# Modulation rows split between TensorE and VectorE, and two narrow projections in 32-column groups

## Chip, core and metric

One Trainium2 chip, one core of it. The program is one launch over all inputs, in fp32. The metric is the device time of one execution in microseconds; several executions of the kernel are timed and the median is taken.

## What is computed

A first block (a gated delta rule and a spatial gating unit, then a mixture of experts) and a second block of two layers (forgetting attention, latent attention, each with a mixture of experts), over 512 tokens of 1024 channels. Three pieces of it are touched:

```python
# second block: 2 layers x 6 vectors of 1024, from one vector c
c_act = jax.nn.silu(c)                       # (1, 1024)
mod = c_act @ w_ada[i] + b_ada[i]            # w_ada[i] is (1024, 6144): 50 MB in two layers
sh1, sc1, g1, sh2, sc2, g2 = jnp.split(mod, 6, axis=-1)

# first block: 16 narrow columns of the input projection
proj = x @ w_in                              # a, b: 8 columns each, from 4096
beta = sigmoid(b);  g = -exp(a_log) * softplus(a + dt_bias)

# forgetting attention: 16 narrow columns
f_logit = (h @ fox_w_in)[..., 3 * D:]        # log_f = log_sigmoid(f_logit + b_f)
```

## The kernel before

The program is laid out by hand in phases, and a scheduling layer then orders the instructions of each engine. Engines run their own queue in that order, so an instruction that waits holds up all behind it on its engine. The phase in question is the first mixer (the first 716 us): spatial gating (`sgu`), then the delta rule (`delta`, with a triangular inverse on VectorE, `sgu_out`, and a scan over chunks), then `gated_sum`.

Nearly all matrix products are exact in fp32 by a split: a weight tile `st` is loaded by SyncE's queue, ScalarE writes its high part `wh` (fp32r), GpSimd or VectorE the rest `wl` (L222), and `mm3` (L384 to L386) adds three fp32r products. A step of `weight1` is 24 such matmuls of 512 moving columns (or 48 of 256). Products in plain fp32 also occur, and the profile shows them as two records each, one for each of two passes (L1259, L1614, L1784).

**Modulation** (`modulation`, L1581 to L1620) is a generator that `weight1` advances: 80 calls, every fifth two steps, 96 steps in all. A step handles one 128-row block k of `w_ada` for one of the 12 vectors: a 512 KB tile `ast` (128 x 1024) from SyncE's queue, of which three are in flight (`AHEAD = 3`, three buffers). VectorE forms `acc = ast * ca[k]` at k = 0 (L1607) and `acc += ast * ca[k]` at k = 1 to 7 (L1609), with `ca` = silu(c) down the partitions. After k = 7 two TensorE products of a column of ones sum `acc` over the partitions into one bank of kind "gen" (L1614, in column groups at output partitions 0 and 32), VectorE adds the bias row (L1618) in two parts of one partition each, and ScalarE's queue writes the vector to DRAM (L1619). The load of step n + 3 is issued behind step n, since it reuses that step's buffer.

**Narrow projections** (`narrow`, L686 to L705) load a weight strip, padded to 64 columns in `gates` and 16 in `fox_heads`, split it in two parts, and take 24 products with the strip as the stationary operand; ScalarE copies the result out and four transposes turn it.

**PSUM.** Eight banks, dealt out by kind in rotation. In the first mixer kind "mm" has banks 0 to 5, in `delta` banks 0 to 2. A bank may be written again when its last reader is done: in `delta` that is VectorE for the convolutions (L722) and for `sgu_out` (L628), ScalarE elsewhere.

Of the kernel before, what the change touches and what calls it, by code (L numbers as in the profile page):

```python
# [10 lines left out]
F32 = mybir.dt.float32  # L11
F32R = mybir.dt.float32r
# [3 lines left out]
AF = mybir.ActivationFunctionType  # L16
ALU = mybir.AluOpType
AX = mybir.AxisListType
# [3 lines left out]
P = 128  # L22
D = 1024
KD = D // P
S = 512
NT = S // P
AHEAD = 3
# [4 lines left out]
def f32(ap):  # L32
    return ap.bitcast(F32)
# [89 lines left out]
class Net:  # L123
# [308 lines left out]
    def mixer1(self):  # L432
        nc, tc, io = self.nc, self.tc, self.io
        ctx = ExitStack()
        with ctx:
# [3 lines left out]
            with ExitStack() as c1:  # L439
                self.wpools(c1, 3, ahead=2, size=1024)  # L440
                self.t2s(c1, x=16)
                self.psums(mm=(0, 1, 2, 3, 4, 5), gen=(6, 7))
                x = io["x"][0]
                xin = self.big("xin")
                for t in range(NT):
                    nc.scalar.dma_start(xin[:, t, :], x[t * P:(t + 1) * P, :])
                self.stage()
                self.slots_left = 0
                self.ada = self.modulation(self.pool(c1, "ada", 1))
                self.xT = self.transpose_split([xin[:, t, :] for t in range(NT)], lambda n, d: self.t2("x", d))  # L450
                with ExitStack() as c2:
                    self.t2s(c2, u=8, gt=2)
                    gT = self.sgu()
                    self.delta_consts()
                    with ExitStack() as c3:
                        self.angles(self.pool(c3, "ang", 1, side="right"))
                    self.head_consts()
                    self.logits = Logits(self, self.t2, io["router_group_w"][0], io["router_group_b"][0],
                                         io["router_expert_w"][0], io["router_expert_b"][0], io["ln1_g"][0], None,
                                         io["ln1_b"][0], True)  # L460
                self.psums(mm=(0, 1, 2), sc=(3, 4, 5), gen=(6,), tr=(7,))
                with ExitStack() as c2:
                    self.t2s(c2, kT=8, th=3, e=2, er=2, qv0=4)
                    self.delta(gT)
                self.psums(mm=(0, 1, 2, 3, 4, 5), gen=(6, 7))
                with ExitStack() as c2:
                    self.t2s(c2, sg=8, ysl=4)
                    y = self.gated_sum()
                    for _ in self.ada:
                        pass  # L470
# [212 lines left out]
            last = self.nc.vector.scalar_tensor_tensor(o, o, mv[:, 1:2], b[i], op0=ALU.mult, op1=ALU.add)  # L683
        return last

    def narrow(self, alloc, parts, n, xT):  # L686

        nc = self.nc

        def tile3(name, dt):  # L690
            return alloc(name, dt, KD * n)[:, :KD * n].rearrange("p (k c) -> p k c", k=KD)

        st, wh, wl = tile3("nw", F32), tile3("nwh", F32R), tile3("nwl", F32R)
        nc.gpsimd.memset(st, 0.0)
        for src, o in parts:
            nc.gpsimd.dma_start(st[:, :, o:o + src.shape[1]], src.rearrange("(k p) c -> p k c", p=P))
        self.split(wh, wl, st)
        ps = self.mm_ps()
        self.ws(ps[:n], ([wh[:, k, :] for k in range(KD)], [wl[:, k, :] for k in range(KD)]), 0, n, xT)
        ab = alloc("nab", F32, S)[:n]  # L700
        nc.scalar.activation(ab, ps[:n], AF.Copy)
        pt = self.mm_ps()
        for t in range(NT):
            nc.tensor.transpose(pt[:, t * n:(t + 1) * n], ab[:, t * P:(t + 1) * P], self.ident[:n, :n])
        return pt[:, :NT * n].rearrange("p (t c) -> p t c", t=NT)  # L705


# [29 lines left out]
    def gates(self):  # L737
        nc, io, sc = self.nc, self.io, self.sc
        w_in = io["w_in"][0]
        pv = self.narrow(lambda n, d, m: self.t2("u", d), [(w_in[:, 4096:4104], 0), (w_in[:, 4104:4112], 32)], 64, self.xT)  # L740
        dtb = self.bcast_row(sc, io["dt_bias"][0], 8, "dtb")
        ea = self.bcast_row(sc, io["a_log"][0], 8, "ea")
        self.tc.keep_in_program_order(nc.scalar.activation(ea, ea, AF.Exp))
# [5 lines left out]
        nc.scalar.activation(self.beta, pv[:, :, 32:40], AF.Tanh, scale=0.5)  # L749
# [830 lines left out]
    def modulation(self, ap):  # L1580

        nc, io = self.nc, self.io
        self.mods = self.dr.tile([2, 6, D], F32, name="mods")
        ca = ap.tile([P, KD], F32, name="ca")
        nc.gpsimd.dma_start(ca, io["c_2"][0].rearrange("(k p) -> p k", p=P))
        nc.scalar.activation(ca, ca, AF.Silu)
        steps = [(l, m, k) for l in range(2) for m in range(6) for k in range(KD)]
        tiles = {}

        def load(n):  # L1590

            if n < len(steps):
                l, m, k = steps[n]
                tiles[n] = ap.tile([P, D], F32, tag="ast", name=self.name("ast"), bufs=AHEAD)
                nc.sync.dma_start(tiles[n], io["w_ada_2"][l, k * P:(k + 1) * P, m * D:(m + 1) * D])

        for n in range(AHEAD):
            load(n)
        for n, (l, m, k) in enumerate(steps):
            st = tiles.pop(n)  # L1600
            if k == 0:
                acc = ap.tile([P, D], F32, tag="acc", name=self.name("acc"), bufs=1)
                row = ap.tile([P, 512], F32, tag="row", name=self.name("row"), bufs=1)
                for i in range(2):
                    nc.gpsimd.dma_start(row[32 * i:32 * i + 1, :],
                                        io["b_ada_2"][l:l + 1, m * D + i * 512:m * D + (i + 1) * 512])
                nc.vector.tensor_scalar(acc, st, ca[:, 0:1], None, op0=ALU.mult)  # L1607
            else:
                nc.vector.scalar_tensor_tensor(acc, st, ca[:, k:k + 1], acc, op0=ALU.mult, op1=ALU.add)  # L1609
            load(n + AHEAD)  # L1610
            if k == KD - 1:
                ps = self.ps("gen")
                for i in range(2):
                    nc.tensor.matmul(ps[32 * i:32 * i + 1, :], self.ones[:, 0:1], acc[:, i * 512:(i + 1) * 512],  # L1614
                                     start=True, stop=True)
                for i in range(2):
                    r = slice(32 * i, 32 * i + 1)
                    nc.vector.tensor_tensor(row[r, :], row[r, :], ps[r, :], op=ALU.add)  # L1618
                    nc.scalar.dma_start(self.mods[l, m:m + 1, i * 512:i * 512 + 512], row[r, :])  # L1619
            yield  # L1620

    def mod_row(self, pool, l, m):
# [219 lines left out]
    def fox_heads(self, ctx, l, x, finish, rows, w_in, op):  # L1842
# [17 lines left out]
        with ExitStack() as c2:  # L1860
# [15 lines left out]
            self.logits = self.logits_of(np_, l)  # L1876

            pf = self.narrow(lambda n, d, m: np_.tile([P, m], d, name=self.name(n)),
                             [(w_in[:, 3072:3088], 0)], 16, xT)
# [300 lines left out]
```

## Time and profile before

| | |
|---|---|
| median of 3 timed executions | 2050.21 us (2049.0 to 2052.03) |
| profiled execution | 2048.78 us, of which 2047.0 us is its span |
| granted TensorE clock, mean | 0.944 |
| TensorE busy | 1821.6 us, 89% of the span |
| VectorE busy | 1376.9 us, 67% |
| ScalarE, GpSimd busy | 857.7 us (42%), 522.6 us (26%) |

A busy share counts an engine's instructions from start to end; matmul ends are modelled and overlap the next start, so how fast TensorE proceeds is read from the starts of following rows. Idle time that the profile puts down to a releaser is named in the views of waits. The two passes of an fp32 product are two rows or two counts.

### The profile page before, as it was taken

How to read it: one execution, taken by the hardware profiler on the slowest of the kernel's cores; microseconds unless marked ns; L12 is line 12 of the kernel's file. 1: busy time of each engine (PE TensorE's matmuls, PEld its weight loads, DVE VectorE, ACT ScalarE, POOL GpSimd, SP SyncE). 2: the span in 40 equal slices, each digit the busy share in tenths (PEclk: the TensorE clock that was granted, in tenths of full speed). 3: DMA queues.
4: the chain of work that ended last, by engine and by line, in shares of the span. 5: the costliest groups of instructions: out<-in, count | busy, mean ns of one | idle time of the engine just before them, and what ended most of it. 6: DMA issues, size and time to landing. Idle time of an engine off the chain costs nothing. (4 is left out here: it accounts for less than half of the span.)

```text
span 2047.0 us, 30174 instructions
## 1 busy us (share of the span) xinstructions
PE 1821.6 (89%) x11594; PEld 1531.3 (75%) x11594; DVE 1376.9 (67%) x2482; ACT 857.7 (42%) x1610; POOL 522.6 (26%) x404
## 2 busy tenths in 40 slices
PE   6989987798889985999589999969997799987997
PEld 6878766677777775888478998957886677786885
DVE  2786885767775466565757555567768778566776
ACT  3334311223333223665334546325543376633552
POOL 5342335223434311111310001231214100232212
PEclk9989999899999987999799998979998999998999
DMA  8753456352547563997404111549972410337993
GB/s 233 191 169 128 154 161 213 101 157 95 152 137 231 178 239 133 330 354 259 162 22 124 42 63 44 225 157 343 357 253 100 135 35 21 118 151 282 349 357 142
DMA packets 174728, 363.33 MB, mean 177 GB/s; under 512 B 23086, under 2 KB 114814, under 8 KB 162288
## 3 DMA queue, kind: packets, MB, share of 16 engines
q1 hardware_dynamic: 154544, 317.94, 46.8%
q0 software_dynamic: 16528, 32.83, 4.7%
q10 hardware_dynamic: 3504, 10.54, 1.3%
q8 instruction: 94, 1.54, 0.3%
q14 instruction: 58, 0.48, 0.1%
HBM read 337.45 MB, written 47.25 MB: 188 GB/s over the span
## 5 line engine op out<-in xcount | busy, mean ns | idle before, releaser
L227 ACT ACTIVATE wh<-st 128x1024 fp32r<-128x1024 f32 (+2 forms) x283 | 310.6, 1101 | 304.3 <-PE mm L386 89.9
L222 DVE TENSOR_TENSOR wl<-st,wh 128x1024 fp32r<-128x1024 f32 (+3 forms) x202 | 263.5, 1306 | 87.3 <-ACT wh L227 86.6
L222 POOL TENSOR_TENSOR wl<-st,wh 128x1024 fp32r<-128x1024 f32 (+1 forms) x81 | 209.0, 2585 | 293.7 <-ACT wh L227 236.8
L384 PE MATMUL mm<-wh,xeh 128*128 128x256 f32 x720 | 211.8, 294 | 0.0
L385 PE MATMUL mm<-wl,xeh 128*128 128x256 f32 x720 | 203.6, 283 | 0.0
L386 PE MATMUL mm<-wh,xel 128*128 128x256 f32 x720 | 203.5, 283 | 0.0
L384 PE MATMUL mm<-x,wh 128*128 128x512 f32 x448 | 183.7, 410 | 15.1 <-DVE sy L628 12.8
L386 PE MATMUL mm<-x,wl 128*128 128x512 f32 x448 | 182.8, 408 | 0.0
L385 PE MATMUL mm<-x,wh 128*128 128x512 f32 x448 | 182.3, 407 | 0.0
L1609 DVE SCALAR_TENSOR_TENSOR acc<-ast,ca,acc 128x1024 f32<-128x1024 f32 x84 | 140.2, 1669 | 62.5 <-DMA ast<-in_w_ada_dram 61.5
L1259 PE MATMUL down<-st,hT 128*128 128x512 f32 x384 | 174.3, 596 | 1.9 <-ACT hT L227 1.9
L385 PEld LDWEIGHTS mm<-wl,xeh 128*128 128x128 f32 x720 | 137.9, 191 | 0.7 <-issue 0.7
L384 PEld LDWEIGHTS mm<-wh,xeh 128*128 128x128 f32 x720 | 137.5, 191 | 0.8 <-issue 0.7
L386 PEld LDWEIGHTS mm<-wh,xel 128*128 128x128 f32 x720 | 137.6, 191 | 0.0
L1274 POOL DMA_INDIRECT yd<-ye,rows x42 | 42.2, 1004 | 318.2 <-DVE ye L1271 185.0
L1259 PEld LDWEIGHTS down<-st,hT 128*128 128x128 f32 x384 | 69.1, 190 | 71.5 <-issue 68.9
L384 PEld LDWEIGHTS mm<-x,wh 128*128 128x128 f32 x448 | 87.0, 194 | 38.1 <-issue 19.6
L384 PE MATMUL mm<-wh,fXH 128*128 128x256 f32 x384 | 113.9, 297 | 0.0
L386 PE MATMUL mm<-wh,fXL 128*128 128x256 f32 x384 | 110.3, 289 | 1.8 <-DVE fXL L222 1.8
L385 PE MATMUL mm<-wl,fXH 128*128 128x256 f32 x384 | 111.0, 289 | 0.0
L385 PEld LDWEIGHTS mm<-x,wh 128*128 128x128 f32 x448 | 86.9, 194 | 17.3 <-issue 1.7
L386 PEld LDWEIGHTS mm<-x,wl 128*128 128x128 f32 x448 | 87.3, 195 | 16.2
(558 smaller groups left out, 4660.0 us busy)
## 6 DMA issues: line engine op xcount, KB each, us to landing
ast<-in_w_ada_dram SPq DMA_DIRECT2D x96, 512.0 KB
st<-in_w_in_dram SPq DMA_DIRECT2D x32, 1024.0 KB
st<-in_moe_w_gate_dram SPq DMA_DIRECT2D x32, 1024.0 KB
st<-in_moe_w_up_dram SPq DMA_DIRECT2D x32, 1024.0 KB
st<-in_moe_w_down_dram SPq DMA_DIRECT2D x30, 1024.0 KB
st<-in_expert_w_gate_dram SPq DMA_DIRECT2D x16, 1024.0 KB
st<-in_expert_w_up_dram SPq DMA_DIRECT2D x16, 1024.0 KB
st<-in_expert_w_down_dram SPq DMA_DIRECT2D x15, 1024.0 KB
```

The lines of the kernel that those rows point to most:

```text
L222: rest = eng.tensor_tensor(l, src, f32(h), op=ALU.subtract)
L227: return self.nc.scalar.activation(out, in_, AF.Copy)
L384: mm(out, lh, rh, start=(start and i == 0), stop=False)
L385: mm(out, lh, rl, start=False, stop=False)
L386: last = mm(out, ll, rh, start=False, stop=(stop and i == n - 1))
L1259: self.nc.tensor.matmul(ps[i], hT[:, k * P:(k + 1) * P], w[:, k * D + i * 512:k * D + (i + 1) * 512], start=k == 0, stop=k == 1)
L1274: return self.nc.gpsimd.indirect_dma_start(out=self.yd[:, :], out_offset=bass.IndirectOffsetOnAxis(ap=dst, axis=0), in_=ye, in_offset=None ...
L1609: nc.vector.scalar_tensor_tensor(acc, st, ca[:, k:k + 1], acc, op0=ALU.mult, op1=ALU.add)
```

## The change

The modulation's even blocks (k = 0, 2, 4, 6) go to TensorE: for each, four fp32 matmuls whose stationary operand is `ca[k]` repeated in 32 columns, over 256 moving columns each, into the four 32-partition groups of one bank. That bank (2, kind "ada") is kept for it through the first mixer, so "mm" has five banks there and two in `delta`. The odd blocks stay on VectorE: k = 1 starts `acc` (tensor_scalar), k = 3, 5, 7 add to it. After k = 7 the ones product (now 32 columns, four groups) adds `acc` to the same bank; one VectorE addition over 128 partitions x 256 columns adds the bias, which now comes as a row repeated in each group, and one DMA writes the vector. Only two loads are issued ahead, with three buffers: the load of step n + 2 stands behind step n and reuses the buffer of step n - 1.

`narrow` keeps its strip in fp32, with no split: 32 columns wide for both uses, eight k blocks in two sets of four, each k block of a set in its own column group, over the high and then the low part of x: 16 fp32 matmuls of 512 moving columns in place of 24. The four partial sums are added in the turning step, which becomes four fp32 products with a 128 x 32 selector (made by one VectorE reduction) in place of four transposes.

```diff
-                self.psums(mm=(0, 1, 2, 3, 4, 5), gen=(6, 7))
+                self.psums(mm=(0, 1, 3, 4, 5), gen=(6, 7), ada=(2,))
...
-                self.psums(mm=(0, 1, 2), sc=(3, 4, 5), gen=(6,), tr=(7,))
+                self.psums(mm=(0, 1), sc=(3, 4, 5), gen=(6,), tr=(7,), ada=(2,))
...
-        st, wh, wl = tile3("nw", F32), tile3("nwh", F32R), tile3("nwl", F32R)
+        st = alloc("nw", F32, KD * n)[:, :KD * n].rearrange("p (k c) -> p k c", k=KD)
...
-        self.split(wh, wl, st)
+        sel = alloc("nsel", F32, n)[:, :n]
+        nc.vector.reduce_sum(sel, self.ident.rearrange("p (g c) -> p c g", g=4), axis=AX.X)
         ps = self.mm_ps()
-        self.ws(ps[:n], ([wh[:, k, :] for k in range(KD)], [wl[:, k, :] for k in range(KD)]), 0, n, xT)
-        ab = alloc("nab", F32, S)[:n]
-        nc.scalar.activation(ab, ps[:n], AF.Copy)
+        for k0 in (0, 4):
+            for i, x in enumerate(xT):
+                for g in range(4):
+                    nc.tensor.matmul(ps[n * g:n * g + n, :], st[:, k0 + g, :], f32(x[k0 + g]),
+                                     start=k0 + i == 0, stop=k0 + i == 5)
+        ab = alloc("nab", F32, S)
+        nc.scalar.activation(ab, ps, AF.Copy)
         pt = self.mm_ps()
         for t in range(NT):
-            nc.tensor.transpose(pt[:, t * n:(t + 1) * n], ab[:, t * P:(t + 1) * P], self.ident[:n, :n])
+            nc.tensor.matmul(pt[:, t * n:(t + 1) * n], ab[:, t * P:(t + 1) * P], sel, start=True, stop=True)
...
+        def rows(ps, w, src, start, stop):
+
+            for a in range(4):
+                nc.tensor.matmul(ps[32 * a:32 * a + 32, :], w, src[:, a * 256:(a + 1) * 256], start=start, stop=stop)
+
-        for n in range(AHEAD):
+        for n in range(AHEAD - 1):
             load(n)
...
             if k == 0:
+                ps = self.ps("ada")[:, :256]
+                row = ap.tile([P, 256], F32, tag="row", name=self.name("row"), bufs=2)
...
-                nc.vector.tensor_scalar(acc, st, ca[:, 0:1], None, op0=ALU.mult)
+            if k % 2 == 0:
+                rows(ps, ca[:, k:k + 1].to_broadcast([P, 32]), st, k == 0, False)
+            elif k == 1:
+                nc.vector.tensor_scalar(acc, st, ca[:, k:k + 1], None, op0=ALU.mult)
             else:
                 nc.vector.scalar_tensor_tensor(acc, st, ca[:, k:k + 1], acc, op0=ALU.mult, op1=ALU.add)
-            load(n + AHEAD)
+            load(n + AHEAD - 1)
             if k == KD - 1:
-                ps = self.ps("gen")
-                for i in range(2):
-                    nc.tensor.matmul(ps[32 * i:32 * i + 1, :], self.ones[:, 0:1], acc[:, i * 512:(i + 1) * 512],
-                                     start=True, stop=True)
-                for i in range(2):
-                    r = slice(32 * i, 32 * i + 1)
-                    nc.vector.tensor_tensor(row[r, :], row[r, :], ps[r, :], op=ALU.add)
-                    nc.scalar.dma_start(self.mods[l, m:m + 1, i * 512:i * 512 + 512], row[r, :])
+                rows(ps, self.ones[:, 0:32], acc, False, True)
+                nc.vector.tensor_tensor(row, row, ps, op=ALU.add)
+                nc.scalar.dma_start(self.mods[l, m].rearrange("(a c) -> a c", a=4),
+                                    row.rearrange("(a b) c -> a b c", a=4)[:, 0, :])
```

The scheduling layer orders all engines anew. Three places are shown; `st`, `ast`, `acc`, `sy` and `row` are the tiles named above, `X` and `Y` the inverse matrices, `q` a small operand that GpSimd prepares, `qv` the convolutions, `sc` scan banks, and numbers count buffers.

On TensorE, before, where the first product with X stands (`join`, L933), late in the third convolution's 24 matmuls:

```order
L386 MATMUL mm_3122<-x_183,wl_3027 128x512
L384 MATMUL mm_3122<-x_192,wh_3026 128x512
L385 MATMUL mm_3122<-x_193,wh_3026 128x512
L386 MATMUL mm_3122<-x_192,wl_3027 128x512
L933 MATMUL sc_2746<-X_2722,q_2738 128x128 x4
L384 MATMUL mm_3122<-x_201,wh_3026 128x512
```

The same place now (that product is L937 here, the convolutions are mm_3097, mm_3142, mm_3182):

```order
L385 MATMUL mm_3142<-x_202,wh_2734 128x512
L386 MATMUL mm_3142<-x_201,wl_2735 128x512
L1604 MATMUL ada_3084<-ast_3140,ca 32x256 x4
L1604 MATMUL ada_3084<-ast_3225,ca 32x256 x4
L937 MATMUL sc_2800<-X_2776,q_2792 128x128 x4
L384 MATMUL mm_3182<-x_138,wh_3080 128x512
```

The third convolution moved behind the first product with X, and two modulation blocks, each behind the load of its tile, stand in its place.

On VectorE, before, the rows that lead to the transposes which build X and Y (L912, L913):

```order
L1618 TENSOR_TENSOR row_2469<-row_2469,gen_2688 1x512 x2
L1607 TENSOR_SCALAR acc_3030<-ast_2616,ca 128x1024
L1609 SCALAR_TENSOR_TENSOR acc_3030<-ast_2650,ca,acc_3030 128x1024
L1609 SCALAR_TENSOR_TENSOR acc_3030<-ast_2686,ca,acc_3030 128x1024
L628 SCALAR_TENSOR_TENSOR sy_2643<-sy_2643,mm_2695 128x512
L1609 SCALAR_TENSOR_TENSOR acc_3030<-ast_3035,ca,acc_3030 128x1024
L1609 SCALAR_TENSOR_TENSOR acc_3030<-ast_3038,ca,acc_3030 128x1024
L912 STREAM_TRANSPOSE X_2722<-W 32x32x32 x3
```

And now:

```order
L1625 TENSOR_TENSOR row_2512<-row_2512,ada_2511 128x256
L1619 TENSOR_SCALAR acc_3087<-ast_2741,ca 128x1024
L628 SCALAR_TENSOR_TENSOR sy_2695<-sy_2695,mm_2749 128x512
L1621 SCALAR_TENSOR_TENSOR acc_3087<-ast_3095,ca,acc_3087 128x1024
L916 STREAM_TRANSPOSE X_2776<-W 32x32x32 x3
```

Of four accumulations one is left ahead of the transposes.

On SyncE's queue, before, the loads behind the first three tiles:

```order
L276 DMA st_232<-in_w_in_dram 128x8x256
L1595 DMA ast_253<-in_w_ada_dram 128x1024
L1595 DMA ast_256<-in_w_ada_dram 128x1024
L276 DMA st_310<-in_w_in_dram 128x8x256
L1595 DMA ast_313<-in_w_ada_dram 128x1024
```

And now:

```order
L276 DMA st_232<-in_w_in_dram 128x8x256
L1599 DMA ast_257<-in_w_ada_dram 128x1024
L1599 DMA ast_317<-in_w_ada_dram 128x1024
L1599 DMA ast_380<-in_w_ada_dram 128x1024
L276 DMA st_311<-in_w_in_dram 128x8x256
```

One `ast` load (that of k = 5) went ahead of a weight load; the tile of k = 4, ast_317, is loaded at the same place as before (ast_256) and is now waited for by TensorE.

## Rows read from the trace of the kernel before

**Rows 1.** The page's totals: engine, busy us, share of the span, instructions.
```profile
PE 1821.6 (89%) x11594; PEld 1531.3 (75%) x11594; DVE 1376.9 (67%) x2482; ACT 857.7 (42%) x1610; POOL 522.6 (26%) x404
```
**Rows 2.** Busy us by stretch (x instructions), first mixer, then clock, DMA share, GB/s.
```profile
0.00:150.00 150.00, 122.27 (x725) 106.85 (x726) 93.43 (x147) 49.89 (x77) 67.68 (x69) 0.94 0.74 201
150.00:250.00 100.00, 96.49 (x521) 79.79 (x520) 77.38 (x169) 42.08 (x82) 27.00 (x15) 0.98 0.42 134
250.00:375.00 125.00, 94.89 (x389) 74.33 (x388) 92.66 (x104) 21.65 (x26) 54.64 (x34) 0.88 0.53 168
375.00:620.00 245.00, 222.76 (x1311) 181.62 (x1311) 176.35 (x356) 82.53 (x189) 78.60 (x51) 0.96 0.46 132
620.00:716.00 96.00, 94.22 (x408) 73.60 (x406) 46.61 (x44) 27.53 (x38) 41.55 (x23) 1.00 0.69 217
```
**Rows 3.** TensorE's waits, 20 to 720 us: total us, times, longest.
```profile
PE sc L933 <- POOL q L931: 14.9, 1, 14.9
PE mm L384 <- DVE sy L628: 12.8, 2, 7.9
PE tr L878 <- DVE qv L879: 6.0, 1, 6.0
PE sc L993 <- DVE St L1004: 4.9, 3, 3.2
...
PE tr L975 <- DVE f L1023: 3.3, 1, 3.3
...
PE mm L599 <- ACT u L594: 2.5, 1, 2.5
...
PE mm L384 <- DVE gt L602: 2.3, 1, 2.3
```
**Rows 4.** VectorE's modulation: the page's group, L1618 by line, L1609 in 250 to 375.
```profile
L1609 DVE SCALAR_TENSOR_TENSOR acc<-ast,ca,acc 128x1024 f32<-128x1024 f32 x84 | 140.2, 1669 | 62.5 <-DMA ast<-in_w_ada_dram 61.5
...
L1618 DVE TENSOR_TENSOR row<-row,gen x24: 665/678/681, 69.0 to 709.2; 1x512 f32<-1x512 f32 x24
...
250.00:375.00 125.00, 34.50 (x17) 0.88 0.53 168
```
**Rows 5.** TensorE in order of time: start us, us, around one ones product (L1614).
```profile
706.68 0.40 PE L386 MATMUL mm<-oh,wl 128*128 128x512 f32 x1
707.01 1.03 PE L1614 MATMUL gen<-acc,ones 128*1 128x512 f32 x4
...
708.30 0.40 PE L385 MATMUL mm<-dol,wh 128*128 128x512 f32 x1
```
**Rows 6.** TensorE in order of time: four whole-array fp32 products of 512 columns.
```profile
869.89 3.63 PE L1259 MATMUL down<-st,hT 128*128 128x512 f32 x8
873.36 1.04 PE L1206 MATMUL gen<-ident,xe 128*128 128x128 f32 x8
```
**Rows 7.** TensorE in order of time: first and last of 24 narrow products.
```profile
1062.39 0.39 PE L384 MATMUL mm<-fXH,nwh 128*16 128x512 f32 x1
...
1067.71 0.39 PE L386 MATMUL mm<-fXH,nwl 128*16 128x512 f32 x1
```
**Rows 8.** VectorE in order of time: two late readers of "mm" banks; one TensorE row.
```profile
284.63 0.68 DVE L628 SCALAR_TENSOR_TENSOR sy<-sy,mm 128x512 f32<-128x512 f32 x1
...
290.31 0.68 DVE L628 SCALAR_TENSOR_TENSOR sy<-sy,mm 128x512 f32<-128x512 f32 x1
...
274.78 0.50 PE L384 MATMUL mm<-x,wh 128*128 128x512 f32 x1
```
**Rows 9.** VectorE ahead of X and Y; TensorE's first product with X.
```profile
347.27 6.47 DVE L1609 SCALAR_TENSOR_TENSOR acc<-ast,ca,acc 128x1024 f32<-128x1024 f32 x2 [6.35 <-DMA ast<-in_w_ada_dram]
353.67 5.95 DVE L912 STREAM_TRANSPOSE X<-W 32x1024 f32<-32x1024 f32 x3
...
370.68 2.08 PE L933 MATMUL sc<-X,q 128*128 128x128 f32 x8 [14.90 <-POOL q L931]
```
**Rows 10.** TensorE alone, the stretch of the longer wait on `sy`: clock.
```profile
312.00:324.00 12.00, 4.12 (x12) 0.72 0.75 260
```

More of the change, by code (lines that the diff above doesn't have):

```diff
@@ L464, in mixer1 @@
                     self.delta(gT)
-                self.psums(mm=(0, 1, 2, 3, 4, 5), gen=(6, 7))
+                self.psums(mm=(0, 1, 3, 4, 5), gen=(6, 7), ada=(2,))
                 with ExitStack() as c2:
@@ L684, in normalise, with narrow @@
         return last
[L686 to L691, printed above, removed]
-        st, wh, wl = tile3("nw", F32), tile3("nwh", F32R), tile3("nwl", F32R)
+    def narrow(self, alloc, parts, xT):
+        nc, n = self.nc, 32
+        st = alloc("nw", F32, KD * n)[:, :KD * n].rearrange("p (k c) -> p k c", k=KD)
         nc.gpsimd.memset(st, 0.0)
@@ L739, in gates @@
         w_in = io["w_in"][0]
-        pv = self.narrow(lambda n, d, m: self.t2("u", d), [(w_in[:, 4096:4104], 0), (w_in[:, 4104:4112], 32)], 64, self.xT)
+        pv = self.narrow(lambda n, d, m: self.t2("u", d), [(w_in[:, 4096:4104], 0), (w_in[:, 4104:4112], 8)], self.xT)
         dtb = self.bcast_row(sc, io["dt_bias"][0], 8, "dtb")
@@ L748, in gates @@
         self.beta, g, a, n = small("beta"), small("g"), small("a"), small("nabs")
-        nc.scalar.activation(self.beta, pv[:, :, 32:40], AF.Tanh, scale=0.5)
+        nc.scalar.activation(self.beta, pv[:, :, 8:16], AF.Tanh, scale=0.5)
         nc.vector.tensor_scalar(self.beta, self.beta, 0.5, 0.5, op0=ALU.mult, op1=ALU.add)
@@ L1601, in modulation @@
             if k == 0:
+                ps = self.ps("ada")[:, :256]
+                row = ap.tile([P, 256], F32, tag="row", name=self.name("row"), bufs=2)
+                nc.gpsimd.dma_start(row, io["b_ada_2"][l, m * D:(m + 1) * D].rearrange("(a c) -> a c", a=4)
+                                    .unsqueeze(1).to_broadcast([4, 32, 256]))
                 acc = ap.tile([P, D], F32, tag="acc", name=self.name("acc"), bufs=1)
-                row = ap.tile([P, 512], F32, tag="row", name=self.name("row"), bufs=1)
-                for i in range(2):
-                    nc.gpsimd.dma_start(row[32 * i:32 * i + 1, :],
-                                        io["b_ada_2"][l:l + 1, m * D + i * 512:m * D + (i + 1) * 512])
-                nc.vector.tensor_scalar(acc, st, ca[:, 0:1], None, op0=ALU.mult)
+            if k % 2 == 0:
+                rows(ps, ca[:, k:k + 1].to_broadcast([P, 32]), st, k == 0, False)
+            elif k == 1:
+                nc.vector.tensor_scalar(acc, st, ca[:, k:k + 1], None, op0=ALU.mult)
             else:
                 nc.vector.scalar_tensor_tensor(acc, st, ca[:, k:k + 1], acc, op0=ALU.mult, op1=ALU.add)
-            load(n + AHEAD)
+            load(n + AHEAD - 1)
             if k == KD - 1:
-                ps = self.ps("gen")
-                for i in range(2):
-                    nc.tensor.matmul(ps[32 * i:32 * i + 1, :], self.ones[:, 0:1], acc[:, i * 512:(i + 1) * 512],
-                                     start=True, stop=True)
-                for i in range(2):
-                    r = slice(32 * i, 32 * i + 1)
-                    nc.vector.tensor_tensor(row[r, :], row[r, :], ps[r, :], op=ALU.add)
-                    nc.scalar.dma_start(self.mods[l, m:m + 1, i * 512:i * 512 + 512], row[r, :])
+                rows(ps, self.ones[:, 0:32], acc, False, True)
+                nc.vector.tensor_tensor(row, row, ps, op=ALU.add)
+                nc.scalar.dma_start(self.mods[l, m].rearrange("(a c) -> a c", a=4),
+                                    row.rearrange("(a b) c -> a b c", a=4)[:, 0, :])
             yield
@@ L1878, in fox_heads @@
             pf = self.narrow(lambda n, d, m: np_.tile([P, m], d, name=self.name(n)),
-                             [(w_in[:, 3072:3088], 0)], 16, xT)
+                             [(w_in[:, 3072:3088], 0)], xT)[:, :, 0:16]
             bf = self.bcast_row(np_, io["fox_b_f_2"][0], 16, "bf")
```

## The prediction

> **What bounds the kernel now.** I read the totals first: TensorE is busy for 1821.6 of 2047.0 us, VectorE for 1376.9 [rows 1]. An average over 2 ms hides stages, so next the table by stretch, only over the first mixer, where all modulation work lies [rows 2]. TensorE's column adds up to 630.6 of 716 us, VectorE's to 486.4. TensorE is the bound in four of the five stretches; its idle time in all of them is 716 - 630.6 = 85.4 us, and 30.1 us of it lie in 250 to 375, where VectorE is busy for 92.66 of 125 us. So the third view is TensorE's list of waits [rows 3]: what the change can give back is what stands there with VectorE behind it. The longest wait, 14.9 us, is named after GpSimd's q, but the reader should see the same product in order of time [rows 9]: its other operand X is built by VectorE's transposes, which start at 353.67 behind an accumulation that waited 6.35 us for its tile. So I put it down to VectorE too. The others are `sy` (12.8 in two waits), qv (6.0), St (4.9), f (3.3), u and gt (2.5 and 2.3): 46.7 us with the first.
>
> The modulation on VectorE today is 84 accumulations of 1.669 us, 140.2 us, and 24 row additions of 0.678 us [rows 4]. It is nearly a third of VectorE's work in the mixer, but most of it lies in time in which TensorE has its own work. The change thus loads the engine that sets the pace and relieves one that sets it only in places.
>
> **The change, part by part.** The profiled execution took 2048.78 us, 1.43 below the median of 2050.21. The sum goes on 2048.78 and 1.4 is added at the end.
>
> *A. TensorE's new blocks, +30.* The trace has the same kind of operation: the ones product, two column groups with two passes of 512 columns each. From the product before it to the one two places behind it, starts go from 706.68 to 708.30, 1.62 us [rows 5]. Two ordinary steps would be 2 x 0.231 us (24 narrow products start from 1062.39 to 1067.71, 23 steps [rows 7]), so the ones product costs 1.16 us. A whole-array fp32 pass of 512 columns takes (873.36 - 869.89) / 8 = 0.434 us [rows 6]. One group behind the other would be four passes, 1.74 us; both at once are two, 0.87. The row says at once, and leaves 1.16 - 0.87 = 0.29 us for going in and out of the grouped form. A new block has passes of 256 columns: 2 x 0.217 + 0.29 = 0.73 us if its four groups run at once as the two do. There are 48 even blocks and 12 ones products in the new form, 60 x 0.73 = 43.8; the 12 old ones products go, 12 x 1.16 = 13.9. Net +29.9. All of it lies on TensorE's queue, so all of it counts except where TensorE would have waited anyway; that share I count under E.
>
> The row shows two groups in the time of one; that four do it too is not shown. The Trainium skill, "TensorE: Matmul & The Clock Gate", section "Measured speedup vs the span model", lists three column tiles of 32 at 2.38 times the speed of one, not 3. By that, as an estimate, a block would cost about 0.11 us more and the 60 blocks 7 us more, inside the range below.
>
> *B. Narrow projections, -3.* Now 24 steps of 0.231, 5.55 us each [rows 7]. Then four rounds of four groups, each of two passes of 512: 8 x 0.434 + 0.29 = 3.76 us. That is -1.8 each, -3.6 for both. The turning products with the selector take the place of four transposes; four fp32 products of 128 columns take 1.04 us [rows 6], so their surplus lies between nothing and 1.0 per call, and I take 0.3, as the transposes are fp32 products of the same length. The split of the strip also goes; it lies on engines with slack here.
>
> *C. TensorE waits for loads, +5.* A block on TensorE now waits itself for its tile. VectorE's waits for tiles are 61.5 us in 15 [rows 4]. Behind a waiting block stand TensorE's next weight products, and with them the readers of their banks. The upper bound is half of it, 31 us, since half of the tiles move; the lower bound is none, since VectorE often reaches the tile early while TensorE reaches it in its own order, with at least one set of 24 products (5.5 us) between most blocks. I take 5, near the lower end: the load share is 0.74 in the first stretch and 0.42 to 0.69 afterwards [rows 2], so only the first stretch is crowded, and there some tile should be late. Two loads ahead with three buffers is one less in flight, which is in the bound.
>
> *D. Two banks for "mm" in `delta` instead of three, +4.* A group of products then waits for the reader of the last group but one. The late readers are VectorE's `sy` evacuations: they end at 285.31 and 290.99, while the next group starts at 274.78 [rows 8]. At today's times the first would stop TensorE for 10.5 us, the second for about as long again, so the upper bound is 21 and the lower nothing. I take 4, because both sides move to meet: TensorE comes to this place later by about a third of A (four of the twelve vectors), 10 us, and VectorE earlier by its relief.
>
> *E. VectorE's relief, -21.* VectorE loses 48 accumulations, 80.1 us, and the row additions go from 24 x 0.678 to 12 of half the columns, about 4 us: -92 us of 486. What TensorE gets back of it, wait by wait [rows 3]: of `sy` 12.8 I take 11, since accumulations stand between its evacuations. Behind the longer of these waits the granted clock falls: 312 to 324 has TensorE busy for 4.12 of 12 us at 0.72 [rows 10], so (1 - 0.72) x 2 = 56% of it ran at 1.2 instead of 2.4 GHz, 6.7 us in which half is lost: 3 us. Of u and gt 3 of 4.8. Of the scan (St, f) 4 of 8.2, as these are chains over both engines. Of qv nothing: it sits behind TensorE's and ScalarE's work.
>
> Of the 14.9 for X nothing either, and this is the choice that matters most. The transposes can start about 4 to 6 us earlier, since one accumulation stands ahead of them and not four, and the late tile no longer must. But the order shows that before, most of the third convolution's 24 products ran while X was being built; now they stand behind the first product with X. 21 products of 0.231 are 4.9 us, which cancel the gain. The bounds of E: 8 if only the longer `sy` wait goes; 46.7 - 4.9 + 3 = 45 if all goes.
>
> **Sum:** +30 - 3 + 5 + 4 - 21 = +15 on 2048.78, 2063.8, and 2065 by the median.
>
> **The rivals.**
>
> *R1, faster: VectorE's relief is worth twice that.* For it: in 250 to 375 VectorE is busy for 92.66 us, 34.50 of it accumulations [rows 2, 4], and the 30.1 us of TensorE's idle time there are nearly all waits behind it; half of the accumulations gone is 17 us out of a chain that ends in X. Against it: the chain to X also goes over TensorE. It decides from E = 30 - 3 + 5 + 4 = 36 on. With E at 45 and C and D at 2 each: 30 - 3 + 4 - 45 = -14, 2036.
>
> *R2, the two banks wait.* If VectorE's evacuations do not come earlier, D is 21, not 4: 2065 + 17 = 2082. For it: VectorE only has to keep the same order around its `sy` evacuations. Against it: a third of the work ahead of it is gone.
>
> *R3, four groups do not run at once.* If two go at a time, a block costs twice its passes, +0.434 x 60 = 26, and the narrow products 4 x 2 x 0.434 = 3.5 each, +7: 2065 + 33 = 2098. Against it: the two groups of the ones product do run together [rows 5].
>
> *R4, TensorE stalls on tiles.* C at 31: 2065 + 26 = 2091. For it: 61.5 us of such waits today [rows 4]. Against it: most of them VectorE reaches early.
>
> *R5, no change:* E between 32 and 40 with the rest as above, 2046 to 2054.
>
> **How the numbers follow.** A measurement of this kernel can tell about 0.2%, 4 us, from no change. The forecast, slower with 2054.5 to 2078: 0.38. R1 0.23, R5 0.15, R2 0.10, R4 0.08, R3 0.06. So faster 0.23, same 0.15, slower 0.62. The range leaves out the lower part of R1 (0.08), R3 and half of R4: 2035 to 2092.
>
> **What would show it.** Per block: in the changed trace the starts of TensorE's rows around a 32x256 block should give 0.73 us over the ordinary steps; 1.16 means R3. C shows as TensorE's waits on the DMA of `ast`; D as waits of the convolutions' or `sgu_out`'s first product on `sy` or qv; both are absent if those terms are nothing. VectorE's busy time in 0 to 716 should fall from 486 to about 395. The two `sy` waits should be short, the clock in that stretch near 0.95, and the wait for X about 10 to 15 us still, with the third convolution behind it. A narrow projection should last 3.8 us on TensorE. The prediction is wrong if the first mixer ends before 716 us, which says that the relief was worth more than TensorE's 60 blocks; then the wait at X should have shrunk to a few us.

## The result and the profile after

The changed kernel takes 2111.91 us (median of four executions, 2107.84 to 2120.44) where the kernel before takes 2051.12 in the same comparison: a ratio of 1.0302, with an interval of 1.0281 to 1.0322. That is 58 to 66 us slower. The forecast was 2065, slower by 15; its sign held, its size did not, and the time lies outside the range of 2035 to 2092.

The page's totals of the changed kernel answer to [rows 1]:

```profile
span 2111.0 us, 30956 instructions
PE 1850.7 (88%) x12050; PEld 1535.9 (73%) x12050; DVE 1308.2 (62%) x2422; ACT 860.8 (41%) x1610; POOL 508.6 (24%) x392
```

TensorE has 29 us more to do and VectorE 69 less, yet the span grows by 64. So some 35 us of it is new idle time of TensorE, where the forecast had that time fall. The table by stretch (busy time of TensorE, its weight loads, VectorE, ScalarE, GpSimd; then the clock, the DMA share, GB/s) answers to [rows 2]; the mixer now runs on to about 785:

```profile
0.00:150.00 150.00, 119.10 (x789) 98.58 (x790) 57.14 (x118) 49.24 (x72) 59.65 (x67) 0.98 0.64 181
150.00:250.00 100.00, 81.92 (x466) 67.26 (x465) 64.49 (x136) 35.43 (x69) 20.81 (x10) 0.90 0.46 129
250.00:375.00 125.00, 110.30 (x521) 82.97 (x521) 73.02 (x115) 25.74 (x38) 40.37 (x19) 0.92 0.56 166
375.00:620.00 245.00, 198.82 (x1216) 158.61 (x1215) 150.59 (x282) 66.49 (x147) 74.33 (x54) 0.91 0.46 120
620.00:716.00 96.00, 90.17 (x475) 69.29 (x476) 48.37 (x86) 33.40 (x64) 34.85 (x17) 0.96 0.58 163
```

The stretch 250 to 375, where I looked for both the gain and the rival R1, is fuller on TensorE than before (110 against 95 us). The loss is in 150 to 250 and in 375 to 620, where TensorE idles for 18 and 46 us and its granted clock is 0.90 and 0.91. VectorE's column is lower there too than in [rows 2]: neither engine sets the pace there by its work.

Who waits for whom shows it at once. First the head of TensorE's list, 20 to 780 us, then VectorE's waits for tiles (total us, times, longest; `ada<-ast` is an even block on TensorE):

```profile
PE mm L384 <- DVE sy L628: 13.7, 3, 6.7
PE sc L937 <- POOL q L935: 10.5, 1, 10.5
PE sc L848 <- DVE kT L716: 9.6, 4, 5.4
PE mm L599 <- DVE gt L602: 8.2, 1, 8.2
PE sc L1000 <- DVE V L998: 8.0, 2, 7.7
PE mm L384 <- DVE qv L726: 7.5, 1, 7.5
PE mm L599 <- ACT u L594: 7.1, 1, 7.1
PE ada L1604 <- DMA ast<-in_w_ada_dram: 5.9, 2, 4.9
```
```profile
DVE acc L1621 <- DMA ast<-in_w_ada_dram: 173.4, 24, 15.2
DVE acc L1619 <- DMA ast<-in_w_ada_dram: 5.7, 1, 5.7
```

TensorE itself waits for tiles only 5.9 us. But VectorE, which reads half as many tiles as before, waits for them nearly three times as long: 179 us against the 61.5 of [rows 4]. TensorE's many shorter waits on VectorE (kT, gt, V, qv) are what seems to follow from that. SyncE's queue (`SPq`) points to the cause; its three longest waits before a tile's load:

```profile
SPq L1599 <- DMA ast<-in_w_ada_dram: 161.6, 31, 12.3
SPq L1599 <- DVE acc L1621: 77.1, 26, 13.6
SPq L1599 <- PE ada L1604: 73.7, 25, 12.6
```

The longest, for an earlier tile's transfer, is no sign of the loss: it stands in e1 below with 153.4 us, where the loss is gone. A quarter of the loads (25 of 96) are held until a block on TensorE is done, since that block's tile has the buffer. Pairing the 96 loads with their readers in order of time, an even tile keeps its buffer for 29 us on average, from its issue to the end of its block, and an odd one for 15; in the kernel before any tile kept it for 21. A load takes the buffer that comes free in the scheduling layer's order, and not always that of step n - 1 as said above: the load at 63.88 goes out as an accumulation ends (63.86), while the even tile of three steps earlier lies unread until 69.36. One stretch shows the circle. TensorE's even blocks in order of time, then SyncE's loads, then VectorE:

```profile
132.62 0.64 PE L1604 MATMUL ada<-ast,ca 128*32 128x256 f32 x8
159.96 4.61 PE L599 MATMUL mm<-sgub,v 128*128 128x128 f32 x24 [8.24 <-DVE gt L602]
164.58 0.64 PE L1604 MATMUL ada<-ast,ca 128*32 128x256 f32 x8
```
```profile
138.31 0.38 SPq L276 DMA_DIRECT2D st<-in_w_in_dram  x1
138.74 0.57 SPq L1599 DMA_DIRECT2D ast<-in_w_ada_dram  x1
152.65 0.80 SPq L1599 DMA_DIRECT2D ast<-in_w_ada_dram  x2
```
```profile
149.28 3.34 DVE L1621 SCALAR_TENSOR_TENSOR acc<-ast,ca,acc 128x1024 f32<-128x1024 f32 x1 [11.42 <-DMA ast<-in_w_ada_dram]
158.01 1.28 DVE L1621 SCALAR_TENSOR_TENSOR acc<-ast,ca,acc 128x1024 f32<-128x1024 f32 x1 [5.40 <-DMA ast<-in_w_ada_dram]
159.22 0.68 DVE L602 TENSOR_TENSOR gt<-mm,sgub 128x512 f32<-128x512 f32 x1
```

Between 133 and 164 us TensorE does no block, so the even tile that was loaded at 137.88 keeps its buffer until 165. VectorE's odd tile is loaded at 138.74, behind a weight tile, and lands at 149.28 after a wait of 11.42 us; only when that accumulation ends, at 152.62 (149.28 + 3.34), do the next loads go out (152.65), and VectorE waits again until 158.01. Behind it in its queue stands gt, for which TensorE waits 8.24 us. And TensorE's next block, which would free a buffer, is behind that wait.

### The profile page after: what moved, and what is told of

Its sections match the earlier page's. It is cut to its first block, busy times and chain, and to the rows that moved or that the text cites. A ratio compares the mean times of both kernels' runs of the same rounds, so it can differ in the third digit from the quotient of the medians.

```text
span 2111.0 us, 30956 instructions
## 1 busy us (share of the span) xinstructions
PE 1850.7 (88%) x12050; PEld 1535.9 (73%) x12050; DVE 1308.2 (62%) x2422; ACT 860.8 (41%) x1610; POOL 508.6 (24%) x392
## 5 line engine op out<-in xcount | busy, mean ns | idle before, releaser
L222 POOL TENSOR_TENSOR wl<-st,wh 128x1024 fp32r<-128x1024 f32 (+1 forms) x81 | 199.4, 2464 | 408.0 <-ACT wh L227 393.3
L384 PE MATMUL mm<-x,wh 128*128 128x512 f32 x448 | 189.9, 424 | 22.5 <-DVE sy L628 13.7
L385 PE MATMUL mm<-x,wh 128*128 128x512 f32 x448 | 184.3, 411 | 0.0
L1621 DVE SCALAR_TENSOR_TENSOR acc<-ast,ca,acc 128x1024 f32<-128x1024 f32 x36 | 66.1, 1837 | 173.4 <-DMA ast<-in_w_ada_dram 173.4
```

Of the source, the lines that this page charges most:

```text
L222: rest = eng.tensor_tensor(l, src, f32(h), op=ALU.subtract)
L384: mm(out, lh, rh, start=(start and i == 0), stop=False)
L385: mm(out, lh, rl, start=False, stop=False)
```

## The experiments

The diffs below show the lines that matter; `...` stands for lines left out, and changes that are only named stand in the text.

**e1 to e4: which term is it?** T1 was that the ring of tiles couples the two engines, T2 that TensorE's blocks cost more than I thought, T3 the banks.

e1, from the changed kernel:

```diff
-                rows(ps, ca[:, k:k + 1].to_broadcast([P, 32]), st, k == 0, False)
+                rows(ps, ca[:, k:k + 1].to_broadcast([P, 32]), None, k == 0, False)
...
+                m = f32(self.xT[0][a])[:, 0:256] if src is None else src[:, a * 256:(a + 1) * 256]
...
```

> The changed kernel, but TensorE's even blocks take columns of x that lie in SBUF in place of the tile of w_ada. The even tiles are still loaded and nobody reads them, so the vectors come out without the even rows; TensorE's and VectorE's work is that of the changed kernel. Theory T1 (ring: an even tile keeps its buffer until TensorE's queue reaches its block, 20 to 40 us, so the odd tiles' loads go out late and VectorE stands in its own queue before them, 173 us in 24 waits): VectorE's wait for tiles falls below 90 us and the time by some 38 us, to 2065 to 2085. Theory T2 (TensorE's 60 blocks, 46 us, and little relief): 2105 to 2115. Theory T3 (two mm banks): 2105 to 2115.

2052.72 us, ratio 0.9997 (0.9978 to 1.0016). VectorE's wait for tiles:

```profile
DVE acc L1622 <- DMA ast<-in_w_ada_dram: 71.8, 9, 13.5
```

That takes away the whole loss, more than the 38 us that T1 said. T2 and T3 fall as main causes, and so do the two loads ahead, which e1 keeps. TensorE's busy time up to the end of the mixer (its last product with `oh` or `dol`), in the kernel before, the changed kernel and e1:

```profile
0.00:713.20 713.20, 629.62 (x3344) 0.95 0.56 165
0.00:782.10 782.10, 666.40 (x3788) 0.94 0.54 152
0.00:719.50 719.50, 655.96 (x3788) 0.96 0.58 165
```

The mixer is 63 us shorter in e1 than in the changed kernel; 52 of them are idle time of TensorE (115.7 against 63.5), the rest busy time, at a granted clock of 0.96 instead of 0.94. The waits of TensorE on gt and on V (L1000) are not in its list any more.

TensorE's order is nearly the same: counted in the traces, 43 of the 48 blocks have the same number of TensorE rows ahead of them. VectorE's is not: 27 of its 48 accumulations moved ahead, by up to 96 of its other rows. So e1 cuts the tie between blocks and buffers together with what the scheduling layer makes of that tie, and does not tell the two apart.

e2, from the changed kernel:

```diff
-                rows(ps, ca[:, k:k + 1].to_broadcast([P, 32]), st, k == 0, False)
+                pass
...
-                rows(ps, self.ones[:, 0:32], acc, False, True)
+                rows(ps, self.ones[:, 0:32], acc, True, True)
```

> The changed kernel without TensorE's 48 even blocks; the even tiles are loaded and not read, so the vectors lack the even rows. VectorE's work, the banks and the loads stay. It takes away both the ring's coupling and 48 x 0.76 = 36 us of TensorE. T1: the coupling's 38 and the 36 both go, 2035 to 2045, below the kernel before. T2: only the 36, about 2076. T3: about 2076 too.

2028.38 us, ratio 0.9869 (0.9838 to 0.9900), 20 to 33 us faster than before. That is more than T1 said. Against e1 the 48 blocks cost 0.0128 x 2051 = 26 us (19 to 34), not the 36 of their price: some lie in time in which TensorE would wait.

e3, from the changed kernel:

```diff
-                tiles[n] = ap.tile([P, D], F32, tag="ast", name=self.name("ast"), bufs=AHEAD)
+                odd = k % 2
+                tiles[n] = ap.tile([P, D], F32, tag=("ast0", "ast1")[odd], name=self.name(("aste", "asto")[odd]), bufs=1 + odd)
...
-        for n in range(AHEAD - 1):
+        for n in (0, 1, 3):
...
-            load(n + AHEAD - 1)
+            load(n + (2, 4)[k % 2])
```

> The changed kernel with the same three buffers dealt out apart: one for even tiles, two for odd ones, so that an odd load never waits for a buffer that TensorE holds (loads still share SyncE's queue, in which a waiting even load holds up those behind it). T1: most of the 38 us come back if the queue's order allows it, 2075 to 2095, and VectorE's wait for tiles falls below 110 us. T2 and T3: 2105 to 2115.

2119.74 us, ratio 1.0300 (1.0252 to 1.0349): no gain, against T1 as I had put it. But the wait has changed its place:

```profile
PE ada L1605 <- DMA aste<-in_w_ada_dram: 50.3, 10, 16.3
DVE acc L1622 <- DMA asto<-in_w_ada_dram: 69.8, 11, 13.0
```

VectorE, with two buffers of its own, is nearly back at its old wait of 61.5. TensorE, with one buffer, now waits itself: a load can go out only after the last block, and lands too late for the next.

e4, from the kernel before:

```diff
-                self.psums(mm=(0, 1, 2, 3, 4, 5), gen=(6, 7))
+                self.psums(mm=(0, 1, 3, 4, 5), gen=(6, 7))
...
-                self.psums(mm=(0, 1, 2), sc=(3, 4, 5), gen=(6,), tr=(7,))
+                self.psums(mm=(0, 1), sc=(3, 4, 5), gen=(6,), tr=(7,))
...
```

> The kernel before with five instead of six mm banks, and two instead of three in delta, and nothing else changed; bank 2 stands empty. T3: 2070 to 2090. T1 and T2: the banks cost little, 2050 to 2058.

2061.39 us, ratio 1.0028 (1.0006 to 1.0049): 1 to 10 us. Two waits of [rows 3] grow:

```profile
PE sc L933 <- POOL q L931: 19.5, 1, 19.5
PE mm L384 <- DVE sy L628: 18.1, 4, 7.7
```

**e5 to e8: buffers, and the narrow projections.**

e5, from the changed kernel; it also has one buffer for row in place of two, k = 1 in quarters, and a ones product that reads the quarter four times. e6 is the same with bufs=3, two loads ahead and two buffers for row, and with three buffers in place of four for pt, a tile of the second block:

```diff
-                tiles[n] = ap.tile([P, D], F32, tag="ast", name=self.name("ast"), bufs=AHEAD)
+                tiles[n] = ap.tile([P, D], F32, tag="ast", name=self.name("ast"), bufs=4)
...
-            load(n + AHEAD - 1)
+            load(n + 3)
...
-                acc = ap.tile([P, D], F32, tag="acc", name=self.name("acc"), bufs=1)
+                acc = ap.tile([P, 256], F32, tag="acc", name=self.name("acc"), bufs=1)
...
-                nc.vector.scalar_tensor_tensor(acc, st, ca[:, k:k + 1], acc, op0=ALU.mult, op1=ALU.add)
+                for a in range(4):
+                    nc.vector.scalar_tensor_tensor(acc, st[:, a * 256:(a + 1) * 256], ca[:, k:k + 1], acc, op0=ALU.mult, op1=ALU.add)
...
```

> The changed kernel with four buffers for tiles and three loads ahead. The room comes from acc, which is 256 columns wide here: VectorE adds the four quarters of an odd tile on top of each other in four instructions (so the vectors are not the right sums), and from one buffer less for row. TensorE's blocks and their waits are those of the changed kernel. T1 (buffers that wait for TensorE starve the odd loads): 2060 to 2085. Rival T4 (it is not the number of buffers but the wait of two engines on one queue of loads, whatever its depth): within 10 us of e6, 2100 to 2120.

> The control of e5: the quarter-wide acc in four instructions, with three buffers and two loads ahead as in the changed kernel. All theories: near the changed kernel, 2100 to 2120; VectorE has about 10 us more to do.

e5 2087.18 us, ratio 1.0187 (1.0166 to 1.0208); e6 2093.34, ratio 1.0218 (1.0196 to 1.0241). VectorE's waits, e5 first:

```profile
DVE acc L1623 <- DMA ast<-in_w_ada_dram: 108.1, 20, 14.9
```
```profile
DVE acc L1623 <- DMA ast<-in_w_ada_dram: 148.3, 25, 15.3
```

A fourth buffer that both engines share takes 40 us off VectorE's wait but only 6 us off the time (0 to 13). So the bare number of buffers is not the answer either: with four, an even tile keeps its buffer for 37 us on average and an odd one for 20, with three for 28 and 15, so the tiles that wait for TensorE take up much of what was added. The control itself is 19 us below the changed kernel, against what I had expected, though VectorE has more to do (94.3 us in these instructions against 66.1). The gain lies in the mixer, which ends at 761 instead of 782, so pt is not its cause; VectorE's instructions are ordered otherwise, and I did not find out which of that does it.

e7, from the kernel before:

```diff
-                tiles[n] = ap.tile([P, D], F32, tag="ast", name=self.name("ast"), bufs=AHEAD)
+                tiles[n] = ap.tile([P, D], F32, tag="ast", name=self.name("ast"), bufs=2)
...
-            load(n + AHEAD)
+            load(n + 2)
...
```

> The kernel before, all eight blocks on VectorE, with two buffers for tiles and two loads ahead in place of three. If the ring is tight whoever reads it (a buffer held while its reader is behind is a buffer lost), the time rises by 30 to 70 us, 2080 to 2120, and VectorE's wait for tiles from 61 to over 130 us. If only the reading by two engines makes it tight, it stays below 2065.

2061.54 us, ratio 1.0047 (1.0023 to 1.0071). VectorE's wait for tiles rises from 61.5 to 96.7 us in 29 waits, and that costs about 10 us. Here a ring with one reader bears the loss of a buffer: 35 us more of such waits cost 10 us, where in the changed kernel 118 us more go with some 60.

e8 is the kernel before with the diff's `narrow`, `gates` and its call in the forgetting attention, and nothing else.

> The kernel before with the new narrow projections and nothing else. Term B says -3, so 2047 to 2050; a projection takes 3.8 us of TensorE instead of 5.6. The rival is that its four groups don't run at once, 2054 to 2058.

2049.60 us, ratio 0.9996 (0.9981 to 1.0011): -4 to +2 us, which holds -3 and cannot tell it from nothing. The trace of the changed kernel has a projection's rows (line, count, ns shortest/median/longest, first and last start):

```profile
L702 PE MATMUL mm<-fXH,nw x16: 592/592/617, 1129.9 to 1132.1; 128*32 128x512 f32 x16
L702 PE MATMUL mm<-fXL,nw x16: 592/592/593, 1130.8 to 1133.0; 128*32 128x512 f32 x16
```

From the first start to the last are 3.1 us; with one pass of 0.434 it is 3.5, as the price in B has it without the entry. Two groups at a time would take about twice that: four groups run at once.

**e9 to e11: TensorE's blocks earlier.** Since the even tiles wait for TensorE, I next said that its blocks stand too late in its order (T1'). e9, from the changed kernel:

```diff
-                rows(ps, ca[:, k:k + 1].to_broadcast([P, 32]), st, k == 0, False)
+                with self.tc.high_priority(1000):
+                    rows(ps, ca[:, k:k + 1].to_broadcast([P, 32]), st, k == 0, False)
```

e10 has 300 in place of 1000; e11 puts VectorE's accumulations under the same priority too.

> The changed kernel with TensorE's even blocks given a high priority in the scheduling layer, so that a block stands in TensorE's order as soon as its tile can be there, some 100 to 200 products earlier than in the changed kernel (the order shows 1248 products ahead of the 23rd block there and 1060 to 1180 here). Three buffers, the same work, the same result. T1' (the ring ties VectorE to TensorE: three buffers let VectorE be no more than two steps ahead of TensorE's blocks, which stand late in TensorE's order): VectorE's wait for tiles falls from 173 to below 100 us and the time to 2050 to 2075. T4 (two readers of one ring cost by themselves, wherever the blocks stand): 2100 to 2115, or TensorE itself waits 30 us or more for tiles.

> As e9 with a smaller priority, which moves the blocks ahead by less from the second half of the mixer on and leaves the ones products late. T1': between e9 and the changed kernel, 2055 to 2090, with VectorE's wait for tiles between theirs. T4: 2100 to 2115.

> As e9, and VectorE's odd accumulations have the same priority. T1': VectorE goes ahead of TensorE again in its order, so part of the wait returns: 5 to 25 us above e9. T4: as e9.

2132.27 (ratio 1.0413), 2131.20 (1.0386) and 2132.87 us (1.0407), each with some 0.002 to either side: all slower than the changed kernel, by some 20 us. T1' falls, and what T4 had named, a wait of TensorE for tiles of 30 us or more, is there. In e9:

```profile
PE ada L1604 <- DMA ast<-in_w_ada_dram: 62.8, 15, 9.5
DVE acc L1622 <- DMA ast<-in_w_ada_dram: 134.7, 21, 15.6
```

With its blocks early TensorE comes before its tiles, as in e3, and VectorE still waits more than twice as long as before; its own loads wait for the same three buffers. Where the blocks stand moves waiting from one engine to the other and does not end it.

**e12 to e14: depth for each reader.** What was left: each reader needs buffers of its own, and enough of them (T5), or the common queue of loads is the trouble (T6). e12, from the changed kernel (e13 has one even buffer in place of four, with the loads of e3):

```diff
-                tiles[n] = ap.tile([P, D], F32, tag="ast", name=self.name("ast"), bufs=AHEAD)
+                odd = k % 2
+                tiles[n] = ap.tile([P, (256, D)[odd]], F32, tag=("ast0", "ast1")[odd], name=self.name(("aste", "asto")[odd]), bufs=(4, 2)[odd])
...
-            load(n + AHEAD - 1)
+            load(n + (8, 4)[k % 2])
...
```

> The changed kernel with two rings as in e3, and even tiles cut to their first 256 columns, so that four buffers for them fit beside two for odd tiles. TensorE's block reads the quarter four times: its work and its wait for its own load are those of the changed kernel, the vectors are not the right ones, and an even load is 128 KB. T5 (what costs is that tiles held for TensorE leave too few buffers: depth): as in e1, 2045 to 2070, TensorE's wait for tiles under 10 us and VectorE's under 90. T6 (two queues of work that each wait for loads behind each other on SyncE's queue): 2085 to 2115.

> The control of e12: the same quarter tiles with one buffer for even tiles, as in e3. T5: 2095 to 2115, TensorE's wait for tiles 25 to 50 us (less than e3's, since a load is a quarter). If smaller loads alone are what helps: within 10 us of e12.

e12 2058.16 us, ratio 1.0033 (1.0018 to 1.0049); e13 2097.49, ratio 1.0202 (1.0166 to 1.0239). In e12 TensorE's list has no wait for a tile at all. VectorE's wait and the loads held for TensorE in e12:

```profile
DVE acc L1622 <- DMA asto<-in_w_ada_dram: 81.0, 12, 14.6
SPq L1600 <- PE ada L1605: 149.3, 32, 14.5
```

and both engines' in e13:

```profile
PE ada L1605 <- DMA aste<-in_w_ada_dram: 38.4, 7, 13.8
DVE acc L1622 <- DMA asto<-in_w_ada_dram: 73.6, 11, 15.0
```

The two differ in the number of even buffers and in the even loads ahead that go with it, and by 39 us (35 by the ratios). The orders of the engines are not in it: all but one of the 48 accumulations and all but one of the 48 blocks have the same number of rows of their engine ahead of them in both. T5 holds for rings that are apart: VectorE then waits 70 to 81 us (e3, e12, e13), not far from its old 61.5, and with four even buffers TensorE doesn't wait either. T6 falls as the main cause: loads stand behind TensorE's blocks on SyncE's queue for 149 us in e12, twice as long as in the changed kernel and nearly as long as in e13 (162.4), and e12 is only 4 to 10 us above the kernel before. What they hold up there is loaded far ahead.

e14, from the changed kernel:

```diff
-            if k % 2 == 0:
+            if k % 4 == 0:
```

> The changed kernel with two blocks of eight (k = 0, 4) on TensorE and six on VectorE; same ring, banks and result. T5: fewer tiles are held for TensorE, so the time lies well below the changed kernel, 2060 to 2085. If the cost were TensorE's blocks alone (0.76 us each), it would fall by 24 x 0.76 = 18 and rise by what VectorE gets back: 2090 to 2110.

2100.21 us, ratio 1.0219 (1.0189 to 1.0250), above what T5 gave and within what the blocks' price alone gave: half as many tiles for TensorE take 12 us off (17 by the ratios), and VectorE still waits 133.6 us.

```profile
DVE acc L1621 <- DMA ast<-in_w_ada_dram: 133.6, 25, 14.4
```

As an estimate, 2 to 7 of these are work: 24 blocks less are 18 us by their price or 13 by e1 against e2, and half of the relief, 11, is lost. That leaves some 5 to 15 of the ring's 60 us: its cost is not in proportion to the tiles that TensorE reads. An even tile here keeps its buffer longer, 34 us on average against 29, but that this is the whole reason was not shown; the loss that stays is against T5 as I had put it.

No experiment that still gives the result is faster than the kernel before. e1 and e12, which come close to it (2053 and 2058), leave out the reading of the even tiles or three quarters of their bytes, and e2's 2028 leaves work out.

## Why the prediction was right or wrong

**A, +30: held.** The ones product in the new form, in order of time on TensorE:

```profile
194.42 0.39 PE L386 MATMUL mm<-x,wl 128*128 128x512 f32 x1
194.74 0.64 PE L1604 MATMUL ada<-acc,ones 128*32 128x256 f32 x8
195.30 0.50 PE L384 MATMUL mm<-x,wh 128*128 128x512 f32 x1
195.64 0.39 PE L385 MATMUL mm<-x,wh 128*128 128x512 f32 x1
```

From 194.42 to 195.64 are 1.22 us, less two ordinary steps of 0.231 are 0.76; forecast was 0.73. So 60 blocks less the 12 old products are +32. R3 is out: two groups at a time would have given 1.16. As an estimate from the Trainium skill's table ("TensorE: Matmul & The Clock Gate", "Measured speedup vs the span model"), with its 2.38 times for three column tiles, a block would have been 0.84; the row is nearer to four groups fully at once. On the path the blocks cost less than their price (26 us of 36, e1 against e2).

**B, -3, and D, +4: held within what can be told** (e8 -4 to +2; e4 +1 to +10).

**E, -21: the size held, its parts did not.** e2 has the relief, the banks, the narrow projections and twelve cheaper ones products, and gains 27 us (20 to 33). Taking off B (-3), D (+4 by forecast) and 12 x (0.76 - 1.16) = -5 leaves -23 for E (-16 to -29 by e2's interval). But of the 11 us that were to go at `sy` only 4 went (12.8 to 8.6 in e2's list), and in the changed kernel none (13.7), where the forecast had these waits short. X (14.9 to 10.3) and qv (6.0 to 1.3), forecast at nothing, and St and f (8.2 to 1.8) gave more, and new waits on sg (8.1) and V (6.2) took some back. That the sum came out is in part luck. The clock term of 3 was also too large as worked out: TensorE is busy for only 4.12 of those 12 us [rows 10], so that half speed can cost it at most 2 there. The choice at X came out otherwise in the changed kernel: there the accumulation ahead of the transposes waits 9.44 us for its tile, and the transposes start 34 us later than in [rows 9]:

```profile
385.46 2.39 DVE L1621 SCALAR_TENSOR_TENSOR acc<-ast,ca,acc 128x1024 f32<-128x1024 f32 x1 [9.44 <-DMA ast<-in_w_ada_dram]
387.77 5.85 DVE L916 STREAM_TRANSPOSE X<-W 32x1024 f32<-32x1024 f32 x3
```

**C, +5: the step that failed.** Without the ring the sum was +30 - 3 + 4 - 21 = +10, and e1, which is just that, measured -5 to +3; most of the difference is the 10 us by which the blocks cost less than their price. The rest, some 60 us (the changed kernel against e1), is C. I had asked how long TensorE would wait for its tiles, and took half of VectorE's wait [rows 4] as the upper bound "since half of the tiles move". TensorE's own wait was 5.9 us, as forecast. What I left out is what a buffer does in the hands of a late reader: "two loads ahead with three buffers is one less in flight, which is in the bound" was wrong, for the bound was worked out from the waits of one in-order reader. In the kernel before VectorE empties the ring in the order in which it is filled; now an even tile lies in its buffer until TensorE comes to its block, 29 us against 15 for an odd one, and the odd tiles have fewer buffers to come into. VectorE's waits grew by 118 us (61.5 to 179.1), and as TensorE waits for what stands behind them in VectorE's queue, about half of that came through to the time.

R4 had the right place and the wrong side: it let TensorE stall on tiles, priced at 31. R2 (banks), R3 (groups) and R1 (relief worth twice as much) did not happen.

**What stays open:** why a fourth shared buffer gained only 6 us (e5 against e6) although VectorE's wait fell by 40, why half as many even tiles gained so little (e14), and why the quarter-wide accumulation alone is 19 us below the changed kernel. The order of VectorE's instructions differs in all of these, and I did not separate it; how much of the 60 us in the shared ring comes by way of that order is open too. That four full-size buffers in a ring of TensorE's own would do the same as e12's quarter tiles was not tried, since there is no room for them; quarter tiles alone account for some 20 us (e3 against e13, with one even buffer each).

## What to carry to other kernels

When a second engine becomes a reader of a ring of buffers, don't price its own wait alone: ask how long it keeps a buffer, and who else's load stands behind that. Here two engines that read one shallow ring, each in its own order, waited for each other through it; moving the reads earlier moved waiting from one to the other (e9 to e11), and rings apart helped only when each was deep enough for the distance between load and use (e12 against e3 and e13). If there is no room for these buffers, splitting the work between the engines can cost more than it relieves: here a relief of some 23 us met 26 us of new work on the bound engine and 60 of coupling.

## What was not expected of the hardware

VectorE's accumulation of 128 x 1024, mostly 1.28 us, takes 3.34 and 6.00 us in single cases (at 149.28 and at 131.85 in the changed kernel), and the mean of the 36 is 1837 ns against 1669 for the 84 of before, where one took 7.09:

```profile
131.85 6.00 DVE L1621 SCALAR_TENSOR_TENSOR acc<-ast,ca,acc 128x1024 f32<-128x1024 f32 x1 [3.95 <-DMA ast<-in_w_ada_dram]
```

In the changed kernel all eleven that took over 2 us come right behind a wait for their tile, and the twelve that did not wait took 1.23 to 1.29 us; before, seven of the fourteen over 2 us came behind such a wait. Why is not shown.

A 512 KB tile that VectorE stood waiting for was there 10.5 us after its issue behind a 1 MB weight tile (138.74 to 149.28); from one odd step to the next it is 785 / 48 = 16 us on average. And the granted clock fell to 0.90 and 0.91 in the two stretches in which TensorE idled for 18 of 100 and 46 of 245 us, where it had been 0.98 and 0.96 [rows 2]. The wait for gt, above, shows how (TensorE's busy time, then its granted clock):

```profile
152.00:160.00 8.00, 0.04 (x1) 0.50 0.73 222
160.00:165.00 5.00, 5.00 (x33) 0.65 0.64 169
165.00:182.00 17.00, 16.47 (x94) 1.00 0.26 60
```

While TensorE idles the clock is at 0.50, the level of 1.2 GHz; from 160 to 165, where TensorE is busy throughout, the mean is 0.65, and only then 1.00. Part of the products that follow this wait thus ran at 1.2 GHz, so that it cost more than its own length.
